# A residual kept with its features on the partitions: output products with the weights stationary

## The chip, the cores and the metric

One core of a Trainium2 chip runs the whole program. The metric is the device time of one execution in microseconds (us).

## The reference

Two transformer layers act on a sequence of 256 tokens of width 2048, in float32. The residual `h` is updated six times, each time by an output product, and each stage reads an RMS-normalised `h`:

```python
for l in range(DEPTH):                       # DEPTH = 2
    hn = _rmsnorm(h, norm_mix[l])
    h = h + (_mixer_ab(hn, ...) if l % 2 == 0 else _mixer_c(hn, ...))   # end in @ w_out
    h = h + _cross_attn(_rmsnorm(h, norm_cross[l]), mem_n, w_q_x[l], w_kv_x[l], w_o_x[l])
    h = h + _conv_ffn(_rmsnorm(h, norm_ffn[l]), w_up[l], conv_w[l], conv_b[l], w_down[l])
return _rmsnorm(h, norm_final)
```

The depths of the output products are 2048 (mixer of layer 0), 4096 (retention mixer of layer 1), 512 (each cross-attention) and 5632 (each feed-forward), all onto 2048 features.

## The kernel before

Every weight is split into a high part (rounded to fp32r by ScalarE, line 239) and the rest (VectorE, line 244), and so is every activation (`xhat`, lines 199 to 209; `split`, line 211). A product is the sum of three: high by high, low by high, high by low. `weights` (line 231) loads 1024 weight columns of 128 partitions at a time on SyncE's queue, and four tiles each of raw, high and low parts are in turn. A slab is 128 features of all 256 tokens, tile [128, 512]: high part in columns 0 to 255, low part in 256 to 511.

There are two forms of product. `product_b_steps` (line 269) has the weights stationary: for a slab k and a block j of 128 output features one matmul of 512 columns (line 283, high weights by both parts of the slab) and one of 256 (line 288, low weights by the high part). The result lies with features on the partitions. `product_a_steps` (line 310) has the activations stationary: for a slab and a half t of the tokens three matmuls of 512 columns (lines 318 to 320). The result lies with tokens on the partitions.

The residual `res` (line 346) has tokens on the partitions: two tiles [128, 2048]. All output products (`out_product`, line 633; `mix_out`, line 1068; the last one in `finish`, line 1098) are therefore `product_a`, in four blocks g of 512 features, and `residual` (line 626) adds 512 columns at a time (line 628). The input products need features on the partitions. So in the last output product of a stage `feed` (line 351) queues for each block g eight transposes (line 361) two steps later, and `xhat` reads their PSUM bank. `Norm.add` (line 149) squares 512 columns on ScalarE with a running sum per token; `Norm.column` reduces these on VectorE (line 156), `rsqrt_of` (line 175) takes 12 small VectorE steps more, and `row_steps` spreads the column over partitions by matmuls of line 196, two steps after. The feed-forward works in chunks of hidden slabs (`FFN_CHUNKS`): the up products of a chunk, then the down product of the chunk before.

TensorE's order is that of the program text (`manual_schedule`); the other engines' orders are the scheduler's. Work beside the products is a list of generators, `side`; `run` and `pump` take a step of the first n of them after each step of a product, and this fixes where side work stands in TensorE's order. PSUM has four banks `acc` for products and four banks `bank` for the rest.

## Time and profile before

| | us |
|---|---|
| median of 3 runs | 2802.67 (2801.71, 2802.67, 10016.6) |
| profiled execution | 2802.01 |
| its span, first to last instruction | 2800.2 |
| PE busy | 2787.2 |
| DVE busy | 1918.4 |
| ACT busy | 1474.6 |
| POOL busy | 29.9 |

The span is read as a string of TensorE instructions. Records of matmuls overlap, since their ends are modelled; what one costs in a row of its kind is the distance from one start to the next.

### The profile page before, as it was taken

What the parts mean: (1) busy time and instruction counts of PE and PEld (TensorE: products, weight loads), DVE (VectorE), ACT (ScalarE), POOL (GpSimd) and SP (SyncE); (2) the same over time, 40 slices, a digit from 0 to 9 for tenths busy, and PEclk for the clock granted to TensorE, in tenths of its full rate; (3) what the DMA queues carried; (4) which work ended last, traced back from release to release, by engine and by line L of the source; (5) the groups of instructions that cost most, each with busy time, mean ns of one, the idle gap of its engine ahead of it and who ended that gap; (6) DMA issues with size and microseconds to landing.
All of it is one profiled execution on the core that took longest, in us unless ns stands there. A gap on an engine that the chain in (4) does not pass through costs nothing.

```text
span 2800.2 us, 39767 instructions
## 1 busy us (share of the span) xinstructions
PE 2787.2 (100%) x14766; PEld 2389.5 (85%) x14766; DVE 1918.4 (69%) x3284; ACT 1474.6 (53%) x2218; POOL 29.9 (1%) x211
## 2 busy tenths in 40 slices
PE   9999999999999999999999999999999999999998
PEld 8888888888888888888888888888888888888887
DVE  7766776776767677666665565566767767676766
ACT  6445465655555555454444454444665646454554
POOL 0000000000000000000000000000000000000000
PEclk9999999999999999999999999999999999999999
DMA  9544565555555556555555555565545555555554
GB/s 328 170 133 152 181 211 167 178 196 189 196 190 201 189 196 206 196 178 181 182 181 185 188 181 187 181 209 190 189 165 196 189 199 189 191 198 191 197 188 158
DMA packets 151267, 530.13 MB, mean 189 GB/s; under 512 B 17120, under 2 KB 17792, under 8 KB 151072
## 3 DMA queue, kind: packets, MB, share of 16 engines
q1 hardware_dynamic: 149184, 523.13, 55.2%
q0 software_dynamic: 1024, 2.90, 0.3%
q8 instruction: 115, 1.88, 0.3%
q10 hardware_dynamic: 864, 1.57, 0.2%
q14 instruction: 80, 0.66, 0.1%
HBM read 525.43 MB, written 2.10 MB: 188 GB/s over the span
## 4 chain that ended last, share of the span: by engine, by line
PE 99%; DVE 0%; DMA 0%; issue 0%; ACT 0%; POOL 0%; SPq 0%; DVEq 0%; ACTq 0%
PE acc L283 33%; PE acc L288 17%; PE acc L318 14%; PE acc L320 14%; PE acc L319 14%; PE bank L361 1%; PE bank L1015 1%; PE bank L525 0%; PE bank L517 0%; PE bank L505 0%; PE bank L1037 0%; PE bank L600 0%; PE bank L610 0%; PE bank L998 0%; PE bank L515 0%; PE bank L526 0%
## 5 line engine op out<-in xcount | busy, mean ns | idle before, releaser
L244 DVE TENSOR_TENSOR t<-t,t 128x1024 fp32r<-128x1024 f32 (+1 forms) x1080 | 1168.4, 1095 | 548.9 <-ACT t L239 502.7
L239 ACT ACTIVATE t<-t 128x1024 fp32r<-128x1024 f32 x954 | 1004.7, 1057 | 707.8 <-PE acc L320 502.2
L283 PE MATMUL acc<-t,t 128*128 128x512 f32 x4096 | 965.1, 391 | 0.9 <-DVE t L203 0.9
L283 PEld LDWEIGHTS acc<-t,t 128*128 128x128 f32 x4096 | 757.5, 188 | 154.3 <-DVE t L203 1.2
L318 PE MATMUL acc<-t,t 128*128 128x512 f32 (+1 forms) x1792 | 699.9, 391 | 0.0
L320 PE MATMUL acc<-t,t 128*128 128x512 f32 (+1 forms) x1792 | 694.8, 388 | 0.0
L319 PE MATMUL acc<-t,t 128*128 128x512 f32 (+1 forms) x1792 | 694.4, 387 | 0.0
L288 PEld LDWEIGHTS acc<-t,t 128*128 128x128 f32 x4096 | 490.0, 188 | 12.1 <-DVE t L244 0.6
L288 PE MATMUL acc<-t,t 128*128 128x256 f32 x4096 | 496.8, 278 | 0.0
L320 PEld LDWEIGHTS acc<-t,t 128*128 128x128 f32 x1792 | 336.4, 188 | 69.3
L318 PEld LDWEIGHTS acc<-t,t 128*128 128x128 f32 x1792 | 336.6, 188 | 67.5
L319 PEld LDWEIGHTS acc<-t,t 128*128 128x128 f32 x1792 | 336.7, 188 | 67.1
L904 ACT ACTIVATE t<-acc 128x256 f32<-128x256 f32 x176 | 65.6, 373 | 251.8 <-PE acc L283 251.8
L907 DVE TENSOR_TENSOR t<-acc,t 128x256 f32<-128x256 f32 x176 | 74.0, 421 | 155.2 <-ACT t L904 155.2
L910 ACT ACTIVATE t<-t,t 128x256 f32<-128x256 f32 x176 | 103.9, 590 | 1.1
L628 DVE TENSOR_TENSOR t<-t,acc 128x512 f32<-128x512 f32 x148 | 95.2, 680 | 1.8 <-PE acc L1132 1.8
L213 ACT ACTIVATE t<-t 128x256 fp32r<-128x256 f32 x88 | 36.1, 410 | 94.3 <-DVE t L929 94.3
L912 DVE SCALAR_TENSOR_TENSOR t<-t,t,t 128x256 f32<-128x256 f32 x176 | 84.1, 478 | 1.5
L911 DVE SCALAR_TENSOR_TENSOR t<-t,t,t 128x256 f32<-128x256 f32 x176 | 84.2, 479 | 0.2 <-issue 0.2
L337 ACT ACTIVATE t<-acc 128x256 f32<-128x256 f32 x80 | 29.9, 374 | 96.4 <-PE acc L283 96.0
L908 DVE TENSOR_TENSOR t<-t,t 128x256 f32<-128x256 f32 x176 | 74.4, 422 | 3.0
L339 DVE TENSOR_TENSOR t<-acc,t 128x256 f32<-128x256 f32 x80 | 33.2, 418 | 60.1 <-ACT t L337 60.1
(227 smaller groups left out, 1204.4 us busy)
## 6 DMA issues: line engine op xcount, KB each, us to landing
t<-in_w_up_dram SPq DMA_DIRECT2D x352, 512.0 KB, 3.3
t<-in_w_in_c_dram SPq DMA_DIRECT2D x192, 512.0 KB, 3.4
t<-in_w_down_dram SPq DMA_DIRECT2D x176, 512.0 KB, 3.3
t<-in_w_in_ab_dram SPq DMA_DIRECT2D x76, 512.0 KB, 4.0
t<-in_w_out_c_dram SPq DMA_DIRECT2D x64, 512.0 KB, 3.3
t<-in_w_out_ab_dram SPq DMA_DIRECT2D x32, 512.0 KB, 4.3
t<-in_w_kv_x_dram SPq DMA_DIRECT2D x32, 512.0 KB, 3.9
t<-in_w_q_x_dram SPq DMA_DIRECT2D x16, 512.0 KB, 3.2
```

The costliest lines, as they stand in the source:

```text
L239: act.activation(hi[:, 0 : m * ncol], raw[:, 0 : m * ncol], AF.Copy)
L244: dve.tensor_sub(lo[:, at[i] : at[i] + (j - i) * ncol], raw[:, c], hi[:, c].bitcast(F32))
L283: pe.matmul(acc[j], parts[k - k0][0][:, j * P : (j + 1) * P], xs[k], start=(k == 0), stop=(end and k == n - 1))
L288: pe.matmul(acc[j][:, 0:S], parts[k - k0][1][:, j * P : (j + 1) * P], xs[k][:, 0:S], start=False, stop=(end and k == n - 1))
L318: pe.matmul(o, xh, hi, start=(k == 0), stop=False)
L319: pe.matmul(o, xh, lo, start=False, stop=False)
L320: pe.matmul(o, xl, hi, start=False, stop=(k == n - 1))
L628: dve.tensor_add(part(t, g), part(t, g), acc)
L908: dve.tensor_mul(u[:, 2:], t, norm.r)
L910: act.activation(c, u[:, 2:], AF.Identity, bias=cp[:, 3, j : j + 1], scale=cp[:, 2, j : j + 1])
L911: dve.scalar_tensor_tensor(c, u[:, 1 : S + 1], cp[:, 1, j : j + 1], c, op0=ALU.mult, op1=ALU.add)
L912: dve.scalar_tensor_tensor(c, u[:, 0:S], cp[:, 0, j : j + 1], c, op0=ALU.mult, op1=ALU.add)
```

## The change

The residual has features on the partitions throughout: eight tiles [128, 512], two slabs each (`slab`). The output products of 8 slabs and more go to `product_b_steps` in eight steps p of 256 output features (`weights` of width 256; the host lays the four output weights out so); the two accumulators of each are added to the residual in four additions of 256 columns. The output products of 4 slabs (cross-attention, and the last chunk of layer 1) go to a new form, `product_n`: three matmuls of 256 columns for each slab and block, all into one half bank; the residual is added in one addition of 512 columns. `feed` no longer transposes: `xhat` reads the residual itself. `Norm.add` squares two slabs on ScalarE and sums them on GpSimd (`pool.tensor_add`, two of 128x256 for a step), and `Norm.column` sums over partitions by two TensorE matmuls of one column (`on_columns`). The load of the input in token order, 2 MB, is gone; the first norm reads the residual tiles. The value product of the second four MoBA heads moves behind their query and key products. Layer 0's feed-forward has chunks of 4, 8, 8, 8, 8, 8. `finish` scales the slabs by the final gain, transposes them (32 transposes, 16 of them ahead of the sum over partitions, 16 behind it) and writes all eight blocks after the rsqrt.

```diff
-FFN_CHUNKS = ((6, 6, 8, 8, 8, 8), (8, 8, 8, 8, 8, 4))
+FFN_CHUNKS = ((4, 8, 8, 8, 8, 8), (8, 8, 8, 8, 8, 4))
...
-    "w_out_ab": cols(0, D, 512),
...
+    "w_out_ab": cols(0, D, 256),
...
-        def add(self, t, g):
-            junk = new([P, 512], F32, "p", 7)
-            act.activation(junk, part(t, g), AF.Square, accum_out=self.sq[:, 4 * t + g : 4 * t + g + 1])
+            self.total, self.first = new([P, S], F32, "total", 1), True
+        def add(self, p):
+            sq = new([P, 512], F32, "p", 7)
+            act.activation(sq, res[p], AF.Square)
+            if self.first:
+                pool.tensor_add(self.total, sq[:, 0:S], sq[:, S:])
+            else:
+                pool.tensor_add(self.total, self.total, sq[:, 0:S])
+                pool.tensor_add(self.total, self.total, sq[:, S:])
+            self.first = False
...
-            v = small(2)
-            dve.tensor_reduce(v, self.sq.rearrange("p (t i) -> p t i", t=2), axis=AX.X, op=ALU.add)
-            self.c = rsqrt_of(v, D, c)
+            self.c = rsqrt_of(on_columns(self.total)[:, 0:2], D, c)
...
+    def on_columns(*sums):
...
         for t in range(2):
-            pe.matmul(b[:, t : t + 1], sums[:, t * P : (t + 1) * P], ones[:, 0:1], start=True, stop=True)
-        return rsqrt_of(b[:, 0:2], n)
+            for i, x in enumerate(sums):
+                pe.matmul(b[:, t : t + 1], x[:, t * P : (t + 1) * P], ones[:, 0:1], start=(i == 0), stop=(i == len(sums) - 1))
+        return b
...
-        n = n or len(xs)
-        for i, ks in enumerate(groups or (range(0, 8), range(8, 16))):
+        n, fine = n or len(xs), groups is None
+        for i, ks in enumerate(groups or [range(k, min(k + 8, n)) for k in range(0, n, 8)]):
...
+    def product_n(ws, xs, accs, evac):
+        parts = [next(ws) for _ in xs]
+        for j in range(2):
+            o = accs[j]
+            for k, (hi, lo) in enumerate(parts):
+                for i in range(2):
+                    pe.matmul(o, hi[:, j * P : (j + 1) * P], xs[k][:, i * S : (i + 1) * S], start=(k == i == 0), stop=False)
+            for k, (hi, lo) in enumerate(parts):
+                pe.matmul(o, lo[:, j * P : (j + 1) * P], xs[k][:, 0:S], start=False, stop=(k == len(parts) - 1))
+            evac(j)
...
-    res = [new([P, D]) for _ in range(2)]
-    def part(t, g):
-        return res[t][:, 512 * g : 512 * g + 512]
+    res = [new([P, 2 * S]) for _ in range(ND // 2)]
+    def slab(s):
...
-        def turn(g):
-            yield
-            yield
-            for s in range(4 * g, 4 * g + 4):
-                b = bank()
-                for t in range(2):
-                    pe.transpose(b[:, t * P : (t + 1) * P], res[t][:, s * P : (s + 1) * P], ident)
-                xs[s] = xhat(b[:, 0:S], gains[:, s : s + 1])
-        def f(g):
-            for t in range(2):
-                norm.add(t, g)
-            side.append(turn(g))
+        def f(p):
+            for s in (2 * p, 2 * p + 1):
+                xs[s] = xhat(slab(s), gains[:, s : s + 1])
+            norm.add(p)
...
-        out_product(w_o, os, 0, head_done)
-    def residual(g, done=None):
-        def ev(t, acc):
-            dve.tensor_add(part(t, g), part(t, g), acc)
-            if t and done is not None:
-                done(g)
+        out_product_n(w_o, os, 0, head_done)
+    def residual(p, done=None):
+        def ev(j, acc):
+            r = slab(2 * p + j)
+            dve.tensor_add(r, r, acc[:, 0:S])
+            dve.tensor_add(r, r, acc[:, S:])
+            if j and done is not None:
+                done(p)
         return ev
     def out_product(w, xs, s0, done=None):
-        for g in range(4):
-            run(product_a_steps(w, xs, 512 * g, 512, residual(g, done), s0=s0))
+        for p in range(ND // 2):
+            run(product_b_steps(weights(w, s0, len(xs), 2 * P * p, 2 * P, LOW), xs, residual(p, done)))
+    def out_product_n(w, xs, s0, done):
+        for p in range(ND // 2):
+            acc = acc_bank()
+            def ev(j):
+                if j:
+                    dve.tensor_add(res[p], res[p], acc)
+                    done(p)
+            product_n(weights(w, s0, len(xs), 2 * P * p, 2 * P), xs, [acc[:, 0:S], acc[:, S:]], ev)
+            pump()
...
+            for p in range(ND // 2):
+                norm.add(p)
...
         for quad in range(2):
-            v = [long(), long()]
-            product_a(w, xs, 2048 + quad * 512, 512,
-                      lambda t, acc: act.activation(v[t], acc, AF.Copy, scale=col[:, t : t + 1]))
...
+                moba_pair(4 * quad + 2 * pair, v)
+            if quad == 1:
+                moba_values(quad, v, 4)
...
-    def mix_out(g, os, done):
+    def mix_out(p, os, done):
         w = Weight("w_out_ab", D)
-        ws = chain(weights(w, 8, 8, g * 512, 512), weights(w, 0, 8, g * 512, 512))
-        return product_a_steps(None, os, 0, 512, residual(g, done), ws=ws, n=ND)
+        ws = chain(weights(w, 8, 8, 2 * P * p, 2 * P, LOW), weights(w, 0, 8, 2 * P * p, 2 * P, LOW, 0))
+        return product_b_steps(ws, os, residual(p, done), n=ND)
...
+            norm, zs = Norm(), []
+            for p in range(ND // 2):
+                accs = [acc_bank()] if p < 7 else [acc_bank(), acc_bank()]
...
+                def scaled(s):
+                    act.activation(z[:, s % 2 * S : (s % 2 + 1) * S], slab(s), AF.Copy, scale=gain("final")[:, s : s + 1])
+                def ev(j):
+                    if p == 7:
+                        r = slab(14 + j)
+                        dve.tensor_add(r, r, accs[j][:, 0:S])
+                        act.activation(sq[:, j * S : (j + 1) * S], r, AF.Square)
+                    elif j:
+                        dve.tensor_add(res[p], res[p], accs[0])
+                        norm.add(p)
+                        for s in (2 * p, 2 * p + 1):
+                            scaled(s)
...
+                product_n(weights(w, s0, len(xs), 2 * P * p, 2 * P), xs,
+                          [accs[0][:, 0:S], accs[0][:, S:] if p < 7 else accs[1][:, 0:S]], ev)
+            for s in (14, 15):
+                scaled(s)
...
+            outs = [turned(0, 0, bank()), turned(1, 0, bank()), turned(0, 1, bank()), turned(1, 1, acc_bank())]
+            sums = on_columns(norm.total, sq[:, 0:S], sq[:, S:])[:, 0:2]
...
+            for i in range(8):
+                g, t = divmod(i, 2)
+                if i > 3:
+                    outs.append(turned(t, g, acc_bank() if i < 7 else bank()))
+            for i, b in enumerate(outs):
+                g, t = divmod(i, 2)
+                y = new([P, 512], F32, "xs", 32)
+                if i % 2:
+                    act.activation(y, b, AF.Copy, scale=c[:, t : t + 1])
+                else:
+                    dve.tensor_scalar_mul(y, b, c[:, t : t + 1])
+                (act if i % 2 else nc.sync).dma_start(out[0, t * P : (t + 1) * P, g * 512 : (g + 1) * 512], y)
```

Two places show what moves. Line numbers of the kernel before are those of the listing; of the changed kernel, L249 is the low part of a weight (L244 before), L208 the low part of a slab (L203), L288 and L293 the two matmuls of `product_b_steps` (L283 and L288), L177 the matmul of `on_columns`, L201 that of `on_rows` (L196), and L183 to L194 the rsqrt (L178 to L189).

First, TensorE at the start of the second cross-attention, before: the last matmul of the mixer's output product (L320), the query product, eight transposes in its midst, and the spreading of the norm.

```order
L320 MATMUL acc_18404<-t_18484,t_17884 128x512
L283 MATMUL acc_18508<-t_18236,t_18511 128x512 [waits Activation_49]
...
L288 MATMUL acc_18509<-t_18358,t_18519 128x256
L361 MATMUL bank_18579<-t_63,t_74 128x128 [waits DVE_49]
L361 MATMUL bank_18579<-t_63,t_75 128x128 [waits DVE_49]
...
L288 MATMUL acc_18508<-t_18444,t_18607 128x256 [waits Activation_49]
...
L288 MATMUL acc_18509<-t_18600,t_18613 128x256
L196 MATMUL bank_18633<-t_63,t_18546 128x128 [waits DVE_49]
...
L283 MATMUL acc_18508<-t_18444,t_18606 128x512
```

And with the change; t_13081 is the sum of squares that GpSimd makes, t_19720 the rsqrt.

```order
L293 MATMUL acc_19620<-t_18884,t_19630 128x256
L288 MATMUL acc_19681<-t_19244,t_19684 128x512 [waits DVE_49,PE_49,Activation_49]
...
L288 MATMUL acc_19682<-t_19429,t_19691 128x512
L177 MATMUL bank_19713<-t_61,t_13081 128x1 [waits Pool_49]
...
L293 MATMUL acc_19681<-t_19244,t_19685 128x256
...
L293 MATMUL acc_19682<-t_19673,t_19763 128x256
L201 MATMUL bank_19783<-t_63,t_19720 128x128 [waits DVE_49]
...
L288 MATMUL acc_19681<-t_19487,t_19756 128x512
```

The transposes are gone; a matmul that waits for GpSimd (L177) stands 16 matmuls of 512 columns behind the end of the output product, and L201, which waits for VectorE, 32 matmuls of 256 columns behind it.

Second, VectorE at the same place, before: L156 sums ScalarE's sums, the rsqrt follows as one piece, and weights and slabs stand behind it.

```order
L156 TENSOR_REDUCE t_18540<-t_12292 128x2 [waits Activation_49]
L178 TENSOR_SCALAR t_18542<-t_18540 128x2 [waits DVE_49]
L180 TENSOR_SCALAR t_18544<-t_18542 128x2 [waits DVE_49]
L182 TENSOR_SCALAR t_18546<-t_18544 128x2 [waits DVE_49]
...
L189 SCALAR_TENSOR_TENSOR t_18546<-t_18557,t_18546 128x2 [waits DVE_49]
L244 TENSOR_TENSOR t_18685<-t_18683,t_18684 128x512 [waits DMAHW6_49,PE_49,Activation_49]
L244 TENSOR_TENSOR t_18685<-t_18683,t_18684 128x512
L244 TENSOR_TENSOR t_18692<-t_18690,t_18691 128x1024 [waits DMAHW7_49,PE_49,Activation_49]
L203 SCALAR_TENSOR_TENSOR t_18582<-bank_18579,t_73,t_18582 128x256 [waits Activation_49]
```

And with the change; t_19735 and the like are slabs of the memory.

```order
L208 SCALAR_TENSOR_TENSOR t_19673<-t_81,t_73,t_19673 128x256 [waits Activation_49]
L183 TENSOR_SCALAR t_19716<-bank_19713 128x2 [waits PE_49]
L208 SCALAR_TENSOR_TENSOR t_19789<-t_19735,t_73,t_19789 128x256 [waits Activation_49]
L185 TENSOR_SCALAR t_19718<-t_19716 128x2 [waits DVE_49]
L208 SCALAR_TENSOR_TENSOR t_19792<-t_19735,t_73,t_19792 128x256 [waits Activation_49]
L187 TENSOR_SCALAR t_19720<-t_19718 128x2 [waits DVE_49]
...
L249 TENSOR_TENSOR t_19835<-t_19833,t_19834 128x512 [waits DMAHW6_49,PE_49,Activation_49]
...
L249 TENSOR_TENSOR t_19842<-t_19840,t_19841 128x1024 [waits DMAHW7_49,PE_49,Activation_49]
...
L208 SCALAR_TENSOR_TENSOR t_19864<-t_19787,t_73,t_19864 128x256 [waits Activation_49]
...
L208 SCALAR_TENSOR_TENSOR t_19891<-t_19823,t_73,t_19891 128x256 [waits Activation_49]
L194 SCALAR_TENSOR_TENSOR t_19720<-t_19731,t_19720 128x2 [waits DVE_49]
```

The rsqrt now starts from a TensorE result (L183), and eight slabs of the memory and three low parts of weights stand between its steps. At the starts of the two feed-forwards and of the retention mixer only the three L249 stand between them.

## Rows read from the trace of the kernel before

**Rows 1.** The page of the profiled execution: share of the span by engine (busy us, share, instructions), the granted TensorE clock in 40 slices, and the chain of work that ended last, by engine.

```profile
PE 2787.2 (100%) x14766; PEld 2389.5 (85%) x14766; DVE 1918.4 (69%) x3284; ACT 1474.6 (53%) x2218; POOL 29.9 (1%) x211
...
PEclk9999999999999999999999999999999999999999
...
PE 99%; DVE 0%; DMA 0%; issue 0%; ACT 0%; POOL 0%; SPq 0%; DVEq 0%; ACTq 0%
```

**Rows 2.** All that TensorE waited for in the whole span, longest first: instruction <- releaser, us in total, times, longest.

```profile
PE bank L505 <- DVE t L497: 1.1, 1, 1.1
PE bank L394 <- POOL t L113: 1.0, 1, 1.0
PE acc L283 <- DVE t L203: 0.9, 1, 0.9
PE bank L319 <- DVE t L244: 0.7, 1, 0.7
```

**Rows 3.** The timeline of TensorE from 1290 us (layer 1, inside the retention mixer): start us, us, engine, line, operation, out<-in, count. The first two rows are the first and the last of 54 matmuls of an activations-stationary product that lie one behind the other without a gap; the next three are a weights-stationary product.

```profile
1290.14 0.39 PE L318 MATMUL acc<-t,t 128*128 128x512 f32 x1
...
1302.15 0.39 PE L320 MATMUL acc<-t,t 128*128 128x512 f32 x1
1302.38 3.79 PE L283 MATMUL acc<-t,t 128*128 128x512 f32 x16
1306.01 3.81 PE L288 MATMUL acc<-t,t 128*128 128x256 f32 x32
1309.66 0.60 PE L1037 MATMUL bank<-t,t 128*128 128x128 f32 x4
```

**Rows 4.** The timeline of TensorE at one of the 20 places where four slabs of the residual are transposed (eight transposes, line 361) between two matmuls of the product that goes on; same columns.

```profile
500.66 1.03 PE L361 MATMUL bank<-t,t 128*128 128x128 f32 x8
501.45 0.48 PE L318 MATMUL acc<-t,t 128*128 128x512 f32 x1
501.76 0.39 PE L319 MATMUL acc<-t,t 128*128 128x512 f32 x1
```

**Rows 5.** Groups of instructions of the whole span by line, engine and shape: out<-in, shapes, count | busy us, mean ns of one | idle time of the engine just before them, and what ended it.

```profile
L244 DVE TENSOR_TENSOR t<-t,t 128x1024 fp32r<-128x1024 f32 x822 | 1002.3, 1222 | 480.0 <-ACT t L239 472.7 <-issue 4.8 <-DMA t<-in_mem_dram 1.5
L239 ACT ACTIVATE t<-t 128x1024 fp32r<-128x1024 f32 x948 | 999.9, 1059 | 706.5 <-PE acc L320 502.2 <-PE acc L283 105.4 <-issue 45.0
...
L628 DVE TENSOR_TENSOR t<-t,acc 128x512 f32<-128x512 f32 x148 | 95.2, 680 | 1.8 <-PE acc L1132 1.8
...
L907 DVE TENSOR_TENSOR t<-acc,t 128x256 f32<-128x256 f32 x176 | 74.0, 421 | 155.2 <-ACT t L904 155.2
...
L200 ACT ACTIVATE t<-bank,t 128x256 fp32r<-128x256 f32 x112 | 44.5, 468 | 17.8 <-PE bank L1037 14.0 <-PE bank L361 3.7
...
L151 ACT ACTIVATE t<-t 128x512 f32<-128x512 f32 x56 | 34.7, 620 | 13.8 <-DVE t L628 13.4 <-DMA t<-in_rows_dram 0.2
```

**Rows 6.** Busy time by engine in one stretch, the output product of the first cross-attention: stretch, us, then busy us (and count) of PE, PEld, DVE, ACT, POOL, the granted clock, the DMA share and GB/s.

```profile
488.00:507.00 19.00, 19.00 (x93) 15.83 (x92) 15.18 (x23) 12.84 (x26) 0.00 (x0) 1.00 0.42 144
```

**Rows 7.** The timeline of VectorE at the start of the second cross-attention: the rsqrt of the row norms (lines 156 to 189: first row and last row of its 13 arithmetic steps), and what stands behind it.

```profile
1971.20 0.16 DVE L156 TENSOR_REDUCE t<-t 128x2 f32<-128x8 f32 x1
1971.39 0.17 DVE L178 TENSOR_SCALAR t<-t 128x2 f32<-128x2 f32 x1
...
1973.57 0.16 DVE L189 SCALAR_TENSOR_TENSOR t<-t,t 128x2 f32<-128x2 f32 x1
1973.68 2.43 DVE L244 TENSOR_TENSOR t<-t,t 128x512 fp32r<-128x512 f32 x3
1976.02 1.65 DVE L203 SCALAR_TENSOR_TENSOR t<-bank,t,t 128x256 fp32r<-128x256 f32 x4
```

**Rows 8.** The timeline of VectorE near the start of the program: the end of the angle steps (line 474) and, among them, the last step of the first rsqrt.

```profile
45.82 0.50 DVE L474 TENSOR_SCALAR t<-t 128x256 f32<-128x256 f32 x2
...
46.62 0.16 DVE L189 SCALAR_TENSOR_TENSOR t<-t,t 128x2 f32<-128x2 f32 x1
```

**Rows 9.** The timeline of TensorE there: a matmul of the product of 256 columns, the first matmul of the product of 280 columns, six matmuls later, and one that stands 12 matmuls behind that.

```profile
40.39 0.28 PE L318 MATMUL bank<-t,t 128*128 128x256 f32 x1
...
41.11 0.29 PE L318 MATMUL acc<-t,t 128*128 128x280 f32 x1
...
42.65 0.29 PE L318 MATMUL acc<-t,t 128*128 128x280 f32 x1
```

**Rows 10.** The GpSimd instructions of the kernel with the most data, by line and shape: count | busy us, mean ns of one | idle time before them.

```profile
L801 POOL MEMSET t<- 128x256 f32 x2 | 0.6, 314 | 56.6 <-DVE t L676 28.8 <-DVE t L339 27.8
...
masks.py:199 POOL TENSOR_SCALAR_AFFINE_SELECT t<-t 128x128 f32<-128x128 f32 x1 | 0.3, 282 | 0.0
```

**Rows 11.** The timeline of VectorE at the end of the program: the last addition to the residual, the first step of the last rsqrt, and the last scaling of the result.

```profile
2790.92 0.69 DVE L628 TENSOR_TENSOR t<-t,bank 128x512 f32<-128x512 f32 x1 [0.90 <-PE bank L1132]
...
2792.40 0.21 DVE L1145 TENSOR_SCALAR t<-t,t 128x1 f32<-128x1 f32 x1
...
2793.66 0.88 DVE L1156 TENSOR_SCALAR t<-t,t 128x512 f32<-128x512 f32 x2
```

**Rows 12.** The timeline of TensorE there: its last matmul.

```profile
2790.50 0.39 PE L1132 MATMUL bank<-t,t 128*128 128x512 f32 x1
```

**Rows 13.** The DMA view: what the 16 DMA engines moved, in GB/s, in 40 slices of the span, and the writes of the result by SyncE's and by ScalarE's queue (count, KB each, median us from issue to landing).

```profile
GB/s 328 170 133 152 181 211 167 178 196 189 196 190 201 189 196 206 196 178 181 182 181 185 188 181 187 181 209 190 189 165 196 189 199 189 191 198 191 197 188 158
...
out_dram<-t SPq DMA_DIRECT2D x4, 256.0 KB, 3.1
out_dram<-t ACTq DMA_DIRECT2D x4, 256.0 KB, 3.6
```

More of the change, by code (lines that the diff above doesn't have):

```diff
@@ L297, in product_b_steps @@
                 upper(kj, False)
-                if groups is None:
+                if fine:
                     yield
-                lower(jk if last else kj, last)
+                lower(kj, last)
             if not last:
@@ L860, in moba_head @@
             yield
+            while not v:
+                yield
             o = bank()
```

167 lines of the change are left out of this document (62 added, 105 removed).

## The prediction

> **What bounds the kernel now.** The page first: TensorE is busy 2787.2 us, in 100% of the span, the chain that ended last is TensorE in 99%, and the granted clock stands in the top tenth in all 40 slices [rows 1]. The list of TensorE's waits comes next: nothing above 1.1 us, some 4 us together [rows 2]. So time is saved only by taking work from TensorE's string or from the tail behind it, and lost wherever the change puts a wait into that string. VectorE is busy 1918 us, in 69%, ScalarE in 53%, GpSimd in 1% [rows 1]. The profiled execution took 2802.0 us (span 2800.2), the median is 2802.7, so the sum below is made against 2802.0 and carried over as it is.
>
> **What each edit costs.** Start-to-start distances are used, since a matmul's own time is modelled.
>
> *Matmul forms.* In activations-stationary form 54 matmuls start within 1302.38 - 1290.14 = 12.24 us, 0.2266 each. In weights-stationary form 16 of 512 columns take 3.63 us (0.2269 each) and 32 of 256 take 3.65 us (0.1141) [rows 3]. A slab and 512 features are 6 x 0.2266 = 1.360 us before, 4 x (0.2269 + 0.1141) = 1.364 in `product_b_steps`, 12 x 0.1141 = 1.369 in `product_n`. The output products have 16 + 32 + 4 + 4 + 44 + 44 = 144 slabs, times four blocks 576; 48 of them (three products of four slabs) go to `product_n`, 528 to `product_b_steps`: 528 x 0.004 + 48 x 0.009 = **+2.4 us**. Here 256 columns are taken at the price of the row with the same form.
>
> The Trainium skill ("TensorE: Matmul & The Clock Gate", section "Packing small matmuls — row/col tiling") says that a weight load overlaps running matmuls only where the row group differs; the new form loads oftener, so by that rule it should be far slower. Here it would be refuted by the trace, where a 256-column matmul with its own load starts every 0.114 us.
>
> *Transposes.* At 500.66 us eight start, the next matmul 0.79 us later, and that one holds the following back by 0.31 instead of 0.23 [rows 4]: 0.87 a place. All 160 are in 20 such places: **-17.4 us**.
>
> *Column matmuls.* Ten new ones in five norms, at no more than a transpose's 0.1 us [rows 4]: **+1.0 us**.
>
> *VectorE.* The additions grow from 148 of 512 columns at 0.68 us to some 512 of 256 at 0.42 [rows 5] (lines 628 and, as the nearest, 907), +115 to 135 us in all, so 73% busy. In the stretch of an output product VectorE is busy 15.2 of 19.0 us [rows 6], so I cost this at nothing: the next weights cover it. A step of eight slabs is 8 x 2 x (0.2269 + 0.1141) = 5.46 us of TensorE, and VectorE's two low parts of weights (1.22) and four additions are 4.1. Without the cover of weights made in advance the four additions of a step would be paid, 1.7 us each time.
>
> *Wait at L177.* It stands 16 matmuls, 3.63 us, behind the end of the output product. By then must be done: the release (0.42 us from the last matmul's start to the addition, [rows 11, 12]), four additions of 0.42, two `xhat` on ScalarE of 0.47, a Square of 0.62 [rows 5], and two GpSimd additions. No row shows one. The lower bound is 0.31, a memset of the same size, the upper 2.2 ns a column (282 ns for 128), once for 256 columns 0.56, for two inputs 1.1 [rows 10]; I take 0.6, nearest to the one that also reads. The sum is 0.4 + 1.7 + 0.9 + 0.6 + 1.2 = 4.8 us, some 1.0 too late, at the second cross-attention and, after its shorter steps, at the retention mixer. After a `product_n` one addition of 0.68 replaces the four, and 0.3 is left at each feed-forward. At the first cross-attention two weight copies of 1.06 (L239) stand between the slabs on ScalarE, one waiting for TensorE: 2.7. Together 1.0 + 1.0 + 2.7 + 0.3 + 0.3 = **+5.3 us**. Behind L177 on TensorE stands the low half of the same product; everyone waits.
>
> The Trainium skill ("GPSIMD Engine Reference", section 3.1) gives 4497 ns for an addition of 2048 fp32 columns; an estimate from that page is 0.56 to 0.65 us for 256, and the sum would be the same.
>
> *Wait at L201.* TensorE arrives 3.65 us after L177. VectorE needs the rsqrt, 2.3 us (1971.39 to 1973.68), and three low parts that now stand between its steps, 2.34 together (1973.68 to 1976.02) [rows 7]: 4.65, or 1.0 too late at the retention mixer and both feed-forwards. At the two cross-attentions eight low parts of the memory at 0.41 (four in 1.65) stand there too, of which some fill the latency of the small steps: 3.5 too late each. 3 x 1.0 + 2 x 3.5 = **+10.0 us**.
>
> *Start of the program.* The 280-column product begins at 41.11, 12 of its matmuls take 1.54 us [rows 9], so L177 comes at 42.65 and L201 at 44.2. Its rsqrt ended at 46.62 before [rows 8], when nobody waited yet. Now it begins behind the angle steps, at about 45, and with these and one low part of 840 columns (about 1.0, by 1222 ns for 1024 [rows 5]) ends near 48.6: **+4.4 us**. The 2 MB of rows that are no longer loaded free nothing here, as TensorE had no wait there.
>
> *First step of a cross-attention's output product.* Its last block needs the last head after 6 short matmuls (0.68 us) where 3.4 us of work lay in between; the split takes two operations of about 0.41: 0.5 each, **+1.0 us**.
>
> *Tail.* Before, 9.5 us lay between the end of the last matmul (2790.50 + 0.23) and the end, 6.5 of them behind the first scaling at 2793.66 [rows 11, 12]. Now come 16 transposes (1.6, the last additions beside them), six column matmuls (0.6), the rsqrt as before (2792.40 to 2793.66, 1.26), then the scalings and 2 MB of writes instead of 1. The DMA's busiest slice moved 328 GB/s [rows 13]; 1 MB more takes 3.2. Sum 0.2 + 1.6 + 0.6 + 1.3 + 6.5 + 3.2 = 13.4 less 9.5 and 0.2: **+3.7 us** (from 0, if the first writes start before the rest is scaled and 2 MB flow faster, to +5).
>
> *Sum.* 2.4 - 17.4 + 1.0 + 5.3 + 10.0 + 4.4 + 1.0 + 3.7 = +10.4: **2812 us**.
>
> **Rivals.**
>
> 1. *The new waits stay hidden.* TensorE waits almost nowhere now [rows 2], and hops may be shorter, low parts may run earlier. Against it stands the count of operations on VectorE between L177 and L201. Then -17.4 + 2.4 + 1.0 + 3.7 = -10.3: 2792. Chance 0.25.
>
> 2. *256 columns cost what they cost at the start.* There six matmuls take 0.72 us, 0.120 each [rows 9], against 0.114 [rows 3]. The output products have 528 x 4 + 48 x 12 = 2688 of them: 2688 x 0.006 = +16, 2828. Against it: the rows at 0.120 are of the other form. Chance 0.10.
>
> 3. *GpSimd and VectorE hold each other up.* If each GpSimd addition stops VectorE for its length X, a step that also feeds the next stage takes VectorE 4.7 + 2X (two low parts of weights at the distance of their starts, some 1.15, four additions, two low parts of slabs) against 5.46 us in the products of eight slabs that end a stage (retention mixer, layer 0's feed-forward), and 2.6 + 2X (one, one of 0.68, two) against 2.74 in the three of four slabs; eight steps each, less about 8 us that the four tiles of weights in advance allow. An addition that comes while a low part runs waits half of its 1.22 us [rows 5], twice for each L177: 6 us in all. At X = 0.6 that is 3 x (8 x 1.06 - 8) + 6 = 8 us, 2820; at 0.9 it is 3 x (8 x 1.66 - 8) + 2 x (8 x 1.04 - 8) + 6 and ten longer additions at L177, 3: 26 us, 2838. I write 2829. No row shows both engines at once. Chance 0.17.
> The Trainium skill ("SBUF — State Buffer", section "SBUF: two separate sides") calls the port pair that the two engines share an exclusive lock, held for a whole instruction, also by a VectorE operation with two operands in SBUF. No run here shows it yet; the low parts of weights are such operations.
>
> 4. *Slower by over 2%.* The same mechanism, with additions of over 1.1 us, the upper bound above: at X = 1.15 the products of four slabs pay 3 x (8 x 2.16 - 8) = 28, those of eight 2 x (8 x 1.54 - 8) = 9, the ends 6 + 5: 48 us on 2812, 2860. It decides from X = 1.13 on. Chance 0.06.
>
> The change not doing what it says is excluded for the transposes: the order has none in the residual's place.
>
> **The numbers.** The forecast has 0.42, rivals 1 to 4 have 0.25, 0.10, 0.17 and 0.06. A measurement of this kernel tells about 2%, 56 us, from no change: 2746 and 2858. Faster by that would need four times what the transposes give: 0.01. Slower is rival 4 and little else: 0.06. Within it: 0.93. The forecast's own range is 2804 to 2820 (the two wait terms, 15 us together, off by half). The whole range takes rival 1 with a tail of no cost, 2788, rival 2 and most of rival 3, 2834; what it leaves out is the rest of 3 and rival 4, some 0.15.
>
> **What would show it.** In the changed profile: L177 waiting for GpSimd 5 times, some 5 us; L201 waiting for VectorE, some 14 with the start; GpSimd's additions at a mean of 0.6 us (above 0.9 rival 3 gains); starts of L293 0.114 apart; a tail of 13.2 us from TensorE's last product to the end; granted clock unchanged. Wrong it would be if VectorE or GpSimd holds TensorE in the middle of the output products, or if L177 and L201 do not wait at all.

## The result

| | us | against before |
|---|---|---|
| before, median of 4 (one of them 10016.6) | 2802.19 | |
| changed, median of 4 | 2841.07 | 1.0138, 95% interval 1.0125 to 1.0151 |
| profiled: span before, after | 2800.2, 2840.1 | +39.9 |

Slower by 1.4%, well clear of the scatter, though less than the 2% that the prediction takes as the least change to tell. Forecast were 2812 and a range to 2834. The page after, against [rows 1]: VectorE's share has grown by less than foreseen (71%, not 73%), and GpSimd is busy 121 us instead of 30.

```profile
PE 2801.7 (99%) x16018; PEld 2451.5 (86%) x16018; DVE 2027.2 (71%) x3769; ACT 1478.4 (52%) x2174; POOL 120.9 (4%) x310
```

Where [rows 2] had four waits of about 1 us, the timeline of TensorE now has ten more, all at L177 and L201 (start us, us, engine, line, ..., in brackets the wait and who ended it):

```profile
52.49 1.23 PE L201 MATMUL bank<-t,t 128*128 128x128 f32 x4 [7.00 <-DVE t L194]
...
383.87 1.01 PE L201 MATMUL bank<-t,t 128*128 128x128 f32 x3 [4.27 <-DVE t L194]
...
429.00 0.61 PE L177 MATMUL bank<-t,t 128*128 128x1 f32 x4 [2.04 <-POOL t L156]
...
436.80 0.71 PE L201 MATMUL bank<-t,t 128*128 128x128 f32 x4 [1.79 <-DVE t L194]
...
533.82 0.60 PE L177 MATMUL bank<-t,t 128*128 128x1 f32 x4 [2.24 <-POOL t L156]
...
1260.97 0.61 PE L177 MATMUL bank<-t,t 128*128 128x1 f32 x4 [1.19 <-POOL t L156]
...
1265.99 0.71 PE L201 MATMUL bank<-t,t 128*128 128x128 f32 x4 [0.67 <-DVE t L194]
...
1998.13 0.61 PE L177 MATMUL bank<-t,t 128*128 128x1 f32 x4 [1.16 <-POOL t L156]
...
2005.34 0.71 PE L201 MATMUL bank<-t,t 128*128 128x128 f32 x4 [2.73 <-DVE t L194]
...
2103.99 0.49 PE L177 MATMUL bank<-t,t 128*128 128x1 f32 x3 [2.23 <-POOL t L156]
```

In order: program start, norm of the memory, first cross-attention (two rows), first feed-forward, retention mixer (two), second cross-attention (two), second feed-forward. L177 waits 8.9 us in all, L201 16.5. None of these stands in the middle of an output product.

Behind several of these the clock fell. The stretch view (us from:to, length, busy time and count of PE, PEld, DVE, ACT, POOL, then the granted clock, DMA share, GB/s):

```profile
52.00:56.00 4.00, 3.51 (x15) 3.51 (x16) 2.81 (x11) 0.39 (x1) 0.00 (x0) 0.50 0.97 288
384.00:388.00 4.00, 4.00 (x12) 3.32 (x13) 0.00 (x0) 0.39 (x1) 0.00 (x0) 0.50 0.47 168
430.00:433.00 3.00, 3.00 (x16) 3.00 (x15) 2.70 (x11) 3.00 (x9) 0.10 (x1) 0.50 0.07 27
536.00:538.00 2.00, 2.00 (x11) 2.00 (x11) 1.92 (x5) 0.00 (x0) 0.00 (x0) 0.50 0.06 10
2007.00:2010.00 3.00, 3.00 (x9) 2.35 (x8) 2.13 (x6) 0.38 (x1) 0.28 (x3) 0.50 0.02 10
2106.00:2109.00 3.00, 3.00 (x16) 3.00 (x16) 2.76 (x8) 0.00 (x0) 0.00 (x0) 0.50 0.24 76
2040.00:2050.00 10.00, 10.00 (x57) 8.70 (x56) 6.93 (x20) 7.16 (x15) 0.00 (x0) 1.00 0.46 156
```

Six stretches, 31 us together, ran at half clock (1.2 instead of 2.4 GHz), while TensorE waited or behind it; the last row shows the usual 1.00. Here is the account, from the distances between matmul starts: a distance over 0.5 us above the median of its line and shape counts as a wait, half of what is worked at half clock as lost by the clock. A wait counted so is up to 0.25 us longer than its bracket in the timeline: 7.2 us at the program start, 4.4 at the norm of the memory. The expectations and the waits in the section on the experiments are of this kind.

| us | before | after | difference |
|---|---|---|---|
| waits | 3.2 | 30.4 | +27.2 |
| lost by the clock | 0.0 | 11.8 | +11.8 |
| all other distances | 2786.3 | 2787.7 | +1.4 |
| before the first, behind the last matmul's start | 10.7 | 10.1 | -0.6 |

So TensorE's work is, on balance, as long as before. The 39.9 us (27.2 + 11.8 + 1.4 - 0.6 = 39.8) are waits and what followed them.

### The profile page after: what moved, and what is told of

Same layout as the page of the kernel before. It is cut to its first block, busy times and chain, and to the rows that moved or that the text cites. A ratio compares the mean times of both kernels' runs of the same rounds, so it can differ in the third digit from the quotient of the medians.

```text
span 2840.1 us, 43176 instructions
## 1 busy us (share of the span) xinstructions
PE 2801.7 (99%) x16018; PEld 2451.5 (86%) x16018; DVE 2027.2 (71%) x3769; ACT 1478.4 (52%) x2174; POOL 120.9 (4%) x310
## 3 DMA queue, kind: packets, MB, share of 16 engines
q0 software_dynamic: 704, 1.85, 0.2%
## 5 line engine op out<-in xcount | busy, mean ns | idle before, releaser
L249 DVE TENSOR_TENSOR t<-t,t 128x1024 fp32r<-128x1024 f32 (+1 forms) x1216 | 1193.0, 1001 | 425.8 <-ACT t L244 247.7
L288 PE MATMUL acc<-t,t 128*128 128x512 f32 x6208 | 1471.8, 392 | 1.8 <-DVE t L208 1.2
L244 ACT ACTIVATE t<-t 128x1024 fp32r<-128x1024 f32 x962 | 1011.0, 1057 | 668.4 <-PE acc L288 383.0
L288 PEld LDWEIGHTS acc<-t,t 128*128 128x128 f32 x6208 | 1147.9, 188 | 231.4 <-DVE t L208 1.5
L293 PEld LDWEIGHTS acc<-t,t 128*128 128x128 f32 x6208 | 755.4, 189 | 21.4 <-DVE t L249 1.0
L293 PE MATMUL acc<-t,t 128*128 128x256 f32 x6208 | 764.8, 279 | 0.2 <-DVE t L249 0.2
L336 PE MATMUL acc<-t,t 128*128 128x512 f32 (+1 forms) x672 | 262.0, 390 | 0.0
L338 PE MATMUL acc<-t,t 128*128 128x512 f32 (+1 forms) x672 | 259.6, 386 | 0.0
L337 PE MATMUL acc<-t,t 128*128 128x512 f32 (+1 forms) x672 | 259.5, 386 | 0.0
L934 DVE TENSOR_TENSOR t<-acc,t 128x256 f32<-128x256 f32 x176 | 74.1, 421 | 156.3 <-ACT t L931 156.3
L338 PEld LDWEIGHTS acc<-t,t 128*128 128x128 f32 x672 | 127.0, 189 | 25.2
L336 PEld LDWEIGHTS acc<-t,t 128*128 128x128 f32 x672 | 127.2, 189 | 24.8
L337 PEld LDWEIGHTS acc<-t,t 128*128 128x128 f32 x672 | 127.1, 189 | 24.5
L632 DVE TENSOR_TENSOR t<-t,acc 128x256 f32<-128x256 f32 x256 | 97.0, 414 | 17.5 <-PE acc L288 16.7
L633 DVE TENSOR_TENSOR t<-t,acc 128x256 f32<-128x256 f32 x256 | 96.9, 413 | 0.2
L205 ACT ACTIVATE t<-t,t 128x256 fp32r<-128x256 f32 x128 | 57.7, 500 | 45.7 <-DVE t L633 35.2
```

The source lines that it names most:

```text
L244: act.activation(hi[:, 0 : m * ncol], raw[:, 0 : m * ncol], AF.Copy)
L249: dve.tensor_sub(lo[:, at[i] : at[i] + (j - i) * ncol], raw[:, c], hi[:, c].bitcast(F32))
L288: pe.matmul(acc[j], parts[k - k0][0][:, j * P : (j + 1) * P], xs[k], start=(k == 0), stop=(end and k == n - 1))
L293: pe.matmul(acc[j][:, 0:S], parts[k - k0][1][:, j * P : (j + 1) * P], xs[k][:, 0:S], start=False, stop=(end and k == n - 1))
L336: pe.matmul(o, xh, hi, start=(k == 0), stop=False)
L337: pe.matmul(o, xh, lo, start=False, stop=False)
```

## The experiments

Unless said otherwise, the edit is to the changed kernel (2841.07). The kernel before, measured anew beside every group of runs, took 2802.0 to 2802.3 each time.

**fill and fill2: is the clock a price of its own?** Dummy matmuls ahead of L177 and L201:

```diff
+    def filler(b):
+        for _ in range(FILL[0]):
+            pe.matmul(b[:, 3 * P :], ident, ident, start=True, stop=True)
```

> The changed kernel with dummy 128x128 transposes put right ahead of L177 and L201 (20, 22, 12, 12, 22 ahead of L177 in the order of the stages; 64 at the program start, 40 at the norm of the memory, 18, 0, 7, 26, 0 ahead of the others of L201), about as long as TensorE waits there. Theory A: the waits themselves are as long as before, but the granted clock no longer falls behind them, so the 31 us at half clock of the changed kernel go and with them the 12 us that they cost: 2829. Rival: the clock falls for another reason than TensorE standing still there: 2841, and the half-clock stretches are still in the trace.

> As fill, with half as many dummy matmuls (10, 11, 6, 6, 11 ahead of L177; 32, 20, 8, 0, 3, 12, 0 ahead of L201), since one of them took 0.223 us there and not 0.11: now they last about as long as the waits. Theory A, as before: no half-clock stretch, waits nearly gone, the fillers in their place: 2841 less the 12 us that the clock cost: 2829 (2828 to 2832). Rival, the fillers cost what they last in addition: 2840 and more.

fill 2858.6 us, fill2 2832.85 us, 0.9 above theory A's range. In neither does a half-clock stretch remain ahead of the last matmul; fill2, the same places:

```profile
384.00:388.00 4.00, 4.00 (x19) 3.31 (x18) 1.97 (x4) 1.99 (x3) 0.00 (x0) 1.00 0.16 62
...
2106.00:2109.00 3.00, 3.00 (x15) 2.45 (x15) 2.75 (x6) 2.98 (x6) 0.10 (x1) 1.00 0.22 33
```

In fill each dummy took 0.223 us, twice what it was sized for, 53 us in all, so its forecast of 2829 missed; 2840.1 + 53 - 25 (waits) - 12 (clock) gives its span of 2856. In fill2 27 us of dummies replace 23 us of waits, and the kernel that does more work is 8.2 us faster. The clock was a price of its own, and it came from TensorE standing still at these places. With the clock up, L201 of both feed-forwards, which did not wait in the changed kernel, waits 0.7 us in both runs; the step L201 of the sum, below, takes this up.

**start_mem, late, late2: does the place in the string decide?**

```diff
 start_mem:
             norm.column(col)
-            yield
+            for _ in range(5):
+                yield
 (and two more yields ahead of the memory's on_rows)
 late (late2: one yield ahead of column, two behind):
             self.column()
-            yield
-            yield
+            for _ in range(3):
+                yield
 both:
+                if mid and last:
+                    upper(jk[: len(jk) // 2], last)
+                    yield
+                    upper(jk[len(jk) // 2 :], last)
```

> The changed kernel with L201 moved later in TensorE's string at the two places where no residual is at stake: at the program start (four more steps, 48 matmuls of 280 columns, 6 us) and at the norm of the memory (two more steps). Theory A: the two waits of 7.2 and 4.4 us and the two half-clock stretches behind them (5 us together) go: 2824 to 2826. Rival: VectorE is late in any case, and the wait turns up at the next user of the norm (the scaled gates, the tables, the memory's keys): 2835 to 2841.

> The changed kernel with L201 of the five stages one half of a product's last 512-column matmuls (8 of them, 1.8 us) later in TensorE's string; L177 stays. Theory A, the place in the string decides: the L201 waits of 1.96, 0.83 and 2.89 us become 0.2, 0 and 1.1, and the half-clock stretch behind the last goes: 2834 to 2836. Rival, VectorE's chain moves along with the later step (its order is the scheduler's) and the waits stay: 2840 to 2842.

> The changed kernel with both L177 and L201 of the five stages moved later: L177 behind the 16 low matmuls of the first 8 slabs (1.83 us later), L201 behind half of the last 512-column matmuls. Theory A, the place decides: the L177 waits of 2.2, 2.4, 1.3, 1.3, 2.4 become 0.4, 0.6, 0, 0, 0.6, those of L201 0.2, 0, 0, 1.1, 0, and four half-clock stretches at the stages go: 2841 - 8 - 5 - 6 = 2822 (2820 to 2826). Rival, GpSimd and VectorE are late as a whole and the waits come up again at the next user of the norm: 2830 and more.

2830.11, 2836.08 and 2831.22 us: late at the edge of theory A's range, start_mem 4 us above it, and late2 5 us above it, at the rival's figure. In start_mem the memory's wait is gone and the start's is 1.9 instead of 7.2, but the first cross-attention's L201 waits 3.0 instead of 2.0. TensorE's work between L177 and L201 ran at half clock there in the changed kernel and at full clock in start_mem, so TensorE came sooner to the same late norm. In late L201 waits 0, 0 and 1.0 at the three stages, as theory A has it. In late2 the L177 waits shrink from 8.9 to 1.8 (by the brackets), and L201 of the retention mixer no longer waits; at the two cross-attentions L201 waits 2.8 and 3.6, longer than before.

The reason is in the distances. From L177's start TensorE needs some 4.2 us at full clock to reach L201. Where L201 waits, it starts 5.0 us behind L177 at the retention mixer and 7.1 to 7.8 at the cross-attentions: that is how long VectorE takes to the norm. late2 moves both matmuls, and TensorE still has only 4.1 us between them; late moves L201 alone and has 6.1. So the place decides, but at the cross-attentions these moves are too small.

**nopool and dvesum: what do GpSimd's additions cost?**

```diff
 nopool:
-                pool.tensor_add(self.total, self.total, sq[:, 0:S])
-                pool.tensor_add(self.total, self.total, sq[:, S:])
+                pass
 dvesum: all three pool.tensor_add -> dve.tensor_add
```

> The changed kernel, in which GpSimd sums only the first two slabs of each norm (the other additions are left out, so that the norms are not those of the reference). Theory B1, the additions delay L177 by their own length alone (two of 0.9 us): the L177 waits fall from 8.9 to about 1.6 us, two of the three half-clock stretches behind them go, 2829 to 2831; VectorE's operations keep their lengths. Theory B2, GpSimd and VectorE hold each other up: in the stretches that end a stage VectorE's low parts (L208, L249) get shorter as well, by about as much as GpSimd's additions last, all L177 waits go and the L201 waits shrink: 2822 to 2827.

> The changed kernel with the sums of squares on VectorE in place of GpSimd. Theory B2 with a full stop (each GpSimd addition of 0.9 us stops VectorE for as long): an addition on VectorE takes 0.48 and so is the shorter, the ends of stages come earlier: 2825 to 2835. Theory B3, the stop is partial (L208 0.58 in place of 0.49 us on the mean): 1.0 us more VectorE work in each step of the products that end a stage costs more than it saves, as with prodb: 2838 to 2850.

nopool 2823.28 us, dvesum 2835.21. The changed kernel's GpSimd groups (count, busy us, mean ns):

```profile
L156 POOL TENSOR_TENSOR t<-t,t 128x256 f32<-128x256 f32 x48 | 43.9, 915 | 3.7
L155 POOL TENSOR_TENSOR t<-t,t 128x256 f32<-128x256 f32 x48 | 42.6, 888 | 148.3 <-ACT t L151 147.8
```

An addition takes 0.9 us on the mean, not 0.6; the last two of the program (at 2825.15 and 2825.97 us), with no low part beside them, take 0.74. The estimate of 0.56 to 0.65 us that the prediction works out from the Trainium skill's "GPSIMD Engine Reference", section 3.1, is a third below that mean. The group of low parts (two operands in SBUF), first of the changed kernel and then of nopool (where it is line 207):

```profile
L208 DVE SCALAR_TENSOR_TENSOR t<-t,t,t 128x256 fp32r<-128x256 f32 x128 | 70.5, 584 | 3.4 <-ACT t L205 3.4
```

```profile
L207 DVE SCALAR_TENSOR_TENSOR t<-t,t,t 128x256 fp32r<-128x256 f32 x128 | 57.9, 489 | 2.5 <-ACT t L204 2.5
```

So the mean rises from 0.489 to 0.584 us when GpSimd adds. One place, the end of the second cross-attention, shows both sides (all engines' timeline):

```profile
2097.03 1.22 DVE L249 TENSOR_TENSOR t<-t,t 128x1024 fp32r<-128x1024 f32 x1
...
2097.20 1.66 POOL L156 TENSOR_TENSOR t<-t,t 128x256 f32<-128x256 f32 x1
...
2098.17 1.85 DVE L208 SCALAR_TENSOR_TENSOR t<-t,t,t 128x256 fp32r<-128x256 f32 x2
...
2098.93 0.81 POOL L155 TENSOR_TENSOR t<-t,t 128x256 f32<-128x256 f32 x1
2099.82 0.80 POOL L156 TENSOR_TENSOR t<-t,t 128x256 f32<-128x256 f32 x1
2099.94 0.68 DVE L649 TENSOR_TENSOR t<-t,acc 128x512 f32<-128x512 f32 x1
...
2101.68 0.87 DVE L208 SCALAR_TENSOR_TENSOR t<-t,t,t 128x256 fp32r<-128x256 f32 x2
...
2102.22 0.91 POOL L155 TENSOR_TENSOR t<-t,t 128x256 f32<-128x256 f32 x1 [1.60 <-ACT t L151]
```

Two low parts of slabs (L208) take 1.85 us beside the end of one addition and the whole of another, and 0.87 at 2101.68, where the next addition begins only at 2102.22; the addition of 1.66 us runs beside a low part of weights of 1.22. The last addition to the residual (L649) starts 1.0 us later for that. That either engine's work gets longer beside the other's agrees with the exclusive lock of which the Trainium skill's "SBUF — State Buffer", section "SBUF: two separate sides", speaks.

B2 holds in part. Without the additions the L177 waits are gone, the start's wait falls from 7.2 to 4.2 us, the memory's from 4.4 to 2.3, and the low parts of slabs get shorter. But the low parts of weights hardly do (those of 1024 columns take 1.224 us on the mean with the additions and 1.222 without), and L201's waits at the five stages do not shrink: 2.7, 0.7, 0.7, 2.9 and 0.7 instead of 2.0, 0, 0.8, 2.9 and 0. A full stop of VectorE for every addition is not what the runs show: 128 x 0.095 = 12 us on L208 face the 96 additions of 0.9 that nopool leaves out. dvesum is 5.9 us faster than the changed kernel, though each final step gives VectorE about 1 us more, so B3's forecast fails too. Its start waits 4.9 us, its memory 2.9, L177 7.1 in all (by the brackets) instead of 8.9; so the start and the memory gain more than the ends of the stages, of which its expectation spoke.

**prodb: does VectorE bound the steps of the cross-attentions?**

```diff
-        out_product_n(w_o, os, 0, head_done)
+        out_product(w_o, os, 0, head_done)
```

> The changed kernel with the output products of the two cross-attentions in the two-accumulator form (512 and 256 columns) in place of three matmuls of 256 columns; four additions of 256 columns in place of one of 512 on VectorE. Theory C1, only the distance of the matmuls counts (0.120 against 0.114 us): 24 x 0.120 = 2.88 us a step become 2.75, 16 steps, 2 us less: 2839. Theory C2, VectorE bounds these steps: 1.0 us more of additions in each of 16 steps of 2.75 us makes the ends of the two cross-attentions later by 3 to 6 us each, at L177 of the feed-forwards: 2845 to 2852.

2845.81 us: C2 by its number, though not at the place that it named. L177 of the two feed-forwards waits 2.1 us each, no longer than before; L201, without a wait before, now waits 1.3 and 2.9 us. And TensorE waits for low parts of weights within the products (the longest 1.2 us at L293, at 528.09 us), which it does not do there in the changed kernel.

**notrans and forms: the two parts of TensorE's work, in the kernel before.**

```diff
 notrans:
-                b = bank()
-                for t in range(2):
-                    pe.transpose(b[:, t * P : (t + 1) * P], res[t][:, s * P : (s + 1) * P], ident)
-                xs[s] = xhat(b[:, 0:S], gains[:, s : s + 1])
+                xs[s] = xhat(res[s % 2][:, s // 2 * S : (s // 2 + 1) * S], gains[:, s : s + 1])
 forms (out_product of retention mixer and feed-forwards, with additions into res[j]):
-            run(product_a_steps(w, xs, 512 * g, 512, residual(g, done), s0=s0))
+            run(product_b_steps(weights(w, s0, len(xs), 256 * p, 256, LOW), xs, ev))
```

> The kernel before with the 160 transposes left out and nothing in their place (the slabs are read from the wrong places of the residual, so the output isn't the reference's). The prediction's own term: 17.4 us less, 2785. Rival, part of them lies in waits that come up elsewhere: 2788 to 2795.

> The kernel before with the output products of 8 slabs (retention mixer and feed-forwards but for the last chunk; 112 or so slabs) in the weights-stationary form and with four additions of 256 columns a step, all else as before (the sums land in the wrong places of the residual). The prediction's term: 112 x 4 x 0.004 = 2 us more, 2804. By the accounts of the changed kernel's trace (0.2288 and 0.1152 us from start to start): 112 x 4 x 0.0152 = 7 us more, 2809.

notrans: 2791.26 us, in the rival's range, ratio 0.9963 (0.9948 to 0.9978). TensorE's work falls by 17.05 us, as priced, but 5.8 us of it come back as waits. Its longest, at the matmul of the row norms (L196):

```profile
PE bank L196 <- DVE t L189: 5.8, 6, 1.6
```

The transposes had covered VectorE's rsqrt; taking them out makes L196 wait, by itself, at all five stages and at the norm of the memory (there 1.7 us). forms: 2807.46, ratio 1.0018 (1.0009 to 1.0028): 464 blocks (116 slabs) cost 6.2 us of work, 13 ns each, not 4.

**best, nalt, best2, nlow, best3: what is left.** best is late2 with start_mem's kind of moves (seven steps at the start) and with the memory's slabs loaded two steps later; best2 scales the query behind both query products and alternates accumulators:

```diff
-            into(q, acc, norm.r)
+            us.append(halves(acc))
...
+        for q, u in zip(qt, us):
+            dve.tensor_mul(q, u, norm.r)
 nalt, best2 (product_n, two banks):
-        for j in range(2):
-            for k, (hi, lo) in enumerate(parts):
-                for i in range(2):
+        for k, (hi, lo) in enumerate(parts):
+            for i in range(2):
+                for j in range(2):
 nlow, best3:
-            product_n(weights(w, s0, len(xs), 2 * P * p, 2 * P), xs, ...
+            product_n(weights(w, s0, len(xs), 2 * P * p, 2 * P, LOW, 0), xs, ...
```

> late2, with L201 of the program start behind the whole product of 280 columns, L201 of the memory's norm two steps later, and the loads and splits of the memory's slabs two steps later in both cross-attentions. Theory A: nearly no waits and no half-clock stretch, what is left over the kernel before is the slower forms (11 to 12 us), the longer tail (4) and the column matmuls (2), less the transposes (17): 2802 to 2808. Rival as for late2: over 2815.

> The changed kernel in which the three matmuls of 256 columns of the products of four slabs alternate between two accumulators in two banks (before: twelve one after another into one half of a bank); two additions of 256 columns on VectorE in place of one of 512. Theory D1, the 0.120 us from start to start comes from staying in one accumulator: 0.114 to 0.115 as in the other form, 576 matmuls, 3 to 4 us less: 2837. Theory D2, it belongs to short matmuls that load the same weights twice: 0.120 stays, 2841.

> best, with the scaling of the query by the norm put behind both query products of a cross-attention, so that L201 can stand in the second of them (32 matmuls of 512 and 16 of 256 columns behind L177), and with the alternation of nalt. Theory A: the two waits of 2.8 and 3.2 us that are left in best go, and two half-clock stretches with them (3 us): 2807, less what nalt brings: 2802 to 2808. Rival: VectorE with the slabs of the memory is late for the scaling too, and the heads wait: 2812 and more.

> The changed kernel in which the low parts of the weights of the products of four slabs lie 48 columns further in their tile, as those of most other products do. Theory D3, the distance from start to start hangs on where the low weights lie: the low matmuls of these products (L321) go from 0.120 to 0.114 us, 192 of them, 1.2 us less; those of the high weights (L319) keep 0.12. Theory D2, it belongs to this order of short matmuls: all stay at 0.120.

> best2 with the same shift. Theory D3: 1 us less than best2, 2803 to 2804.5; theory D2: as best2, 2804.7.

best: 2815.86, the rival's figure and not theory A's; L201 of the cross-attentions, still some 4.1 us of work behind L177, waits 2.8 and 3.2 us. best2, with 11.5 us between the two: 2804.75, as theory A has it, ratio 1.0010 (1.0001 to 1.0019). All that TensorE waits for in best2, longest first (the views of [rows 2]):

```profile
PE acc L289 <- DVE t L209: 1.2, 1, 1.2
PE bank L515 <- DVE t L507: 1.2, 1, 1.2
PE bank L404 <- POOL t L117: 1.0, 1, 1.0
PE acc L289 <- DVE t L644: 0.6, 1, 0.6
PE bank L178 <- POOL t L156: 0.2, 1, 0.2
```

With L201 a product later the new waits and all half-clock stretches before the last matmul are gone (account: waits 3.4, clock 0.0), and TensorE's other distances are those of the kernel before but for 2 us. nalt: 2838.14, close to D1's 2837, but its short matmuls stay at 0.1209 (L318) and 0.1200 us; D1 falls. Its profiled execution has 6.5 us lost by the clock instead of 11.8 and nothing else that is shorter by more than 1 us. nlow (2843.06, one run): four low matmuls of a product of four slabs, first in the changed kernel (start, us), then in nlow:

```profile
2078.75 0.64 PE L321 MATMUL acc<-t,t 128*128 128x256 f32 x4
2079.23 1.12 PE L319 MATMUL acc<-t,t 128*128 128x256 f32 x8
```

```profile
2078.26 0.62 PE L321 MATMUL acc<-t,t 128*128 128x256 f32 x4
2078.71 1.12 PE L319 MATMUL acc<-t,t 128*128 128x256 f32 x8
```

0.48 us for four become 0.45; the mean of 192 falls from 0.1200 to 0.1136, that of L319 stays 0.1228. D3 holds for the low weights: their place in the tile decides. In the time of nlow the 1.2 us do not show; its waits came out 2.7 us longer. best3: 2804.12, ratio 1.0007 (0.9998 to 1.0016), the same as before, and in the range of D3, but only 0.6 us under best2; in its profiled execution a wait of 2.5 us early in the program (1.4 in best2) has a half-clock stretch behind it again. No form of the changed kernel was faster than the kernel before.

## Why the prediction was wrong

What bounds the kernel and the sign were right, and the two lines were named at which TensorE would wait. The steps of the sum (waits here by the brackets of the timeline):

- **Clock.** "granted clock unchanged" was the step that failed most: 11.8 us. A wait was priced at its own length alone; in fill2 and best2, where TensorE hardly stands still at these places, the 11.8 us are gone.
- **Program start, +4.4.** 7.0 were measured. The rsqrt began not at about 45 but at 48.6, and ended not at 48.6 but at 52.4 (VectorE, first and last step):

```profile
48.64 0.15 DVE L183 TENSOR_SCALAR t<-bank 128x2 f32<-128x2 f32 x1
...
52.27 0.16 DVE L194 SCALAR_TENSOR_TENSOR t<-t,t 128x2 f32<-128x2 f32 x1
```

  VectorE is late as a whole: the two angle steps of [rows 8] (line 474, now 477) start at 49.22 instead of 45.82. In nopool they start at 46.12 and the wait is 4.1, nearly the forecast. So the rest is the work of GpSimd for the first norm, which the sum had at nothing here.
- **Norm of the memory.** 4.3 us at L201, in no term. I priced the norms that the diff rewrites, not this one, which the diff only moves. TensorE reaches L201 4.1 us behind the start of the last column sum, over 32 matmuls of 256 columns; before, it took 6.5 us, over 24 matmuls of 512 and eight transposes. And the rsqrt starts late, at 378.69 us, 3.2 us behind that sum. On VectorE it stands behind a low part of the residual that waits for ScalarE:

```profile
378.28 0.48 DVE L208 SCALAR_TENSOR_TENSOR t<-t,t,t 128x256 fp32r<-128x256 f32 x1 [1.68 <-ACT t L205]
378.69 0.15 DVE L183 TENSOR_SCALAR t<-bank 128x2 f32<-128x2 f32 x1
```

- **L177, +5.3.** 8.9 were measured. The retention mixer and the second cross-attention came out nearly as priced (1.2 and 1.2 for 1.0 each), the first cross-attention lower (2.0 for 2.7); the miss is 2.2 instead of 0.3 at each feed-forward, for additions of 0.9 and for the hold-up (rival 3's mechanism, at the ends).
- **L201, +10.0.** 5.2 at the stages: 1.8, 0.7 and 2.7. VectorE's chain was sized rightly: the working has 4.65 us from L177 and 3.5 + 3.65 at the cross-attentions, the runs 5.0 and 7.1 to 7.8. But TensorE needs 4.2 us, not 3.65. And at the first cross-attention and both feed-forwards TensorE went from L177 to L201 at half clock, so that it came 1.6 us later and found the norm ready, or nearly so. The first feed-forward in the changed kernel, and in dvesum, where the clock stayed up at this place:

```profile
533.82 0.60 PE L177 MATMUL bank<-t,t 128*128 128x1 f32 x4 [2.24 <-POOL t L156]
534.29 5.52 PE L293 MATMUL acc<-t,t 128*128 128x256 f32 x32
539.64 0.60 PE L201 MATMUL bank<-t,t 128*128 128x128 f32 x4
```

```profile
528.69 0.61 PE L177 MATMUL bank<-t,t 128*128 128x1 f32 x4 [1.75 <-DVE t L156]
...
533.71 0.71 PE L201 MATMUL bank<-t,t 128*128 128x128 f32 x4 [0.66 <-DVE t L194]
```

  So about half of the 4.8 us by which this term was too high are waits that were rightly foreseen and that the half clock hid: start_mem, at full clock, has 2.85 instead of 1.8 at the first cross-attention, and 0.66 at each feed-forward is what dvesum's row shows.
- **Matmul forms, +2.4.** About 10.5: 13 ns for each of 528 blocks (7, by the run forms), and 0.120 us, not 0.114, for the 576 matmuls of `product_n` (3.5), which is rival 2 for those alone. The 16 matmuls of 512 columns in [rows 3] were quicker than most: the means over the changed kernel's matmuls at full clock are 0.2288 (512 columns) and 0.1152 (256).
- **Transposes, -17.4.** 17.05 in notrans: right, but they had covered the rsqrt, as the same run shows.
- **Column matmuls, +1.0.** 2.2, since each is two instructions of 0.11 us on TensorE (x4 in the rows of L177, for two column sums).
- **Tail, +3.7.** 4.2 (13.92 us from the last product's last start, 2826.15, to the end, against 9.73). Nearly right.
- **First step of the output products, +1.0.** Right: the first eight matmuls of each cross-attention's output product take 1.5 us (504.19 to 505.69), the eight of every later step 0.96, 1.1 us for both.

```profile
504.19 1.67 PE L319 MATMUL acc<-t,t 128*128 128x256 f32 x8
505.69 0.64 PE L321 MATMUL acc<-t,t 128*128 128x256 f32 x4
```

Of the 29 us by which the sum fell short, the clock makes 11.8, the forms 8, the waits 7.5 (27.2 against 5.3 + 10.0 + 4.4) and the small terms the rest.

Rival 1 is refuted, rival 4 too. Rival 3 gives 2838 for additions of 0.9 us, close to what came, but this is luck: 16 us of it lie in steps of the four-slab products, where TensorE did not wait, and the clock is not in it. Its mechanism is real at the start and at the ends of the stages: without the additions the kernel takes 17.8 us less (nopool), waits and clock together. That the moves alone explain waits and clock is shown by best2, which differs from the changed kernel in where steps stand, when the query is scaled and the order within `product_n`, whose effect nalt bounds. What stays open: why the products' mean distance is 13 ns a block above the other form (the place of operands, shown for L321, is argued for the rest), and why the clock fell behind some waits and not behind others; nalt waits 2.9 us from 1999.6 us on without a fall, where the changed kernel falls.

## What to carry to other kernels

Work on the busiest engine can be the cover of another engine's chain: before taking it out, write down for each matmul that waits on a chain what stands between the source and it, in us, and what the chain takes. Price a wait of TensorE also by the granted clock behind it, and look at what stands behind that wait: at half clock TensorE comes later to its next wait and can hide it. And look at the norms and side work that the diff doesn't touch but whose steps get shorter.

## What the runs showed of the hardware

TensorE's clock went to half behind waits of 2 to 7 us in a kernel that is otherwise 99% busy, and dummy matmuls in the wait kept it up (fill2). GpSimd additions of 128x256 float32 took 0.74 us with no low part beside them and 0.9 on the mean; VectorE's low parts of slabs, with all operands in SBUF, rose beside them from 0.489 to 0.584 us on the mean, while its additions to the residual with one operand in PSUM (L649) took 0.68, as in nopool (0.69). The distance of two matmuls of 256 columns went from 0.120 to 0.114 us when the low weights moved by 48 columns in their tile (nlow, L321).
